# Dense tiles 1 to 4 instead of 2 to 5 in a hybrid decoder layer with a PEER expert FFN

## The chip, the cores and the metric

The kernel runs on one core of a Trainium2 chip. The metric is the device time of one execution in microseconds. Five engines matter here: TensorE (PE, with its weight loads as PEld), VectorE (DVE), ScalarE (ACT), GpSimd (POOL) and SyncE (SP). Each engine runs its own queue of instructions in order. SP, ACT and POOL also issue DMA transfers.

## What is computed

One decoder layer on 1024 tokens of width 1024, then a final norm. A mixer (mLSTM and stick-breaking attention) and a cross-attention into 256 memory tokens come first. The PEER FFN follows: each token picks 128 experts (8 heads, 16 each) out of 16384, and sums them.

```python
def peer_ffn(h, wq, subkeys, u, v):                 # cut
    q = (xt @ wq).reshape(T, PEER_HEADS, 2, PEER_HALF)
    s = jnp.einsum('thpc,hpnc->thpn', q, subkeys)
    ...                                             # top 16 of 256 candidates in each head
    gates = jax.nn.softmax(best, axis=-1)
    def block(args):                                # 128 tokens
        xb, eb, gb = args
        ub = u[eb]
        vb = v[eb]
        act = jax.nn.gelu(jnp.einsum('cd,ced->ce', xb, ub), approximate=False) * gb
        return jnp.einsum('ce,ced->cd', act, vb)
```

`u` and `v` are 16384 rows of 1024 float32 each, 4 KB a row.

## The kernel before, in words

The 1024 tokens are eight tiles of 128. They go through the front (projections, mixers, cross-attention, routing) in five groups, `GROUPS = (1, 2, 2, 1, 2)`: tile 0; tiles 1, 2; tiles 3, 4; tile 5; tiles 6, 7. While one group is in its mixers or in `post`, the projections (`part_a`) and the mixers of the next group are filled in.

After `route`, `topk` (L682) makes a tile's 128 expert numbers `idx` and gates per token. Then there are two ways to compute a tile's experts.

A **gathered** tile (`experts`, L760) runs on POOL and DVE. For each of its 128 slots POOL issues one indirect DMA (L777) that brings one row of `u` for each of the 128 tokens (512 KB) into one of five buffers `uv` (`uvb=5`), DVE multiplies and sums it into `act` (L784), a Gelu and the gate follow, and for each slot a second gather brings the rows of `v`, which DVE adds to `y` (L792). A tile so needs 256 gathers. The `u` gathers run 32 slots ahead of the `v` gathers.

A **dense** tile is computed against all 16384 experts by TensorE. Its gates are first scattered into a matrix `G_scr` in DRAM, zeroed at the start: `topk` issues 128 indirect DMAs (L748), 16 for each of the 8 heads, which add a gate at expert and token. The 16 of one head are declared independent; the first of a head waits until all of the head before it has landed. Then `dense` (L857) goes over 128 blocks of 128 experts for the four dense tiles together (N = 512): `hmat` (L839) loads a block of `u` transposed and makes the activations `h` (24 matmuls, L850), `gpart` loads that block's part of `G_scr` (L875) and multiplies (L876), `vpart` loads the block of `v`, and `ypart` (L896) adds to seven PSUM banks and, for the eighth, through `h` to `y8` in SBUF (L899). The loads of `G_scr` wait for the last scatter of all dense tiles. `split` (L832) makes high and low parts (L834 on ACT, L836 on DVE). The activations may run `ring=12` blocks ahead.

At the end of each tile `finish` (L802) adds the residual, norms and stores.

The order of the instructions on each engine is fixed when the program is built: the tile framework's planner (`schedule_with_timeline_sim=True`) lays all instructions out on a modelled time line, with priority by their place in the program, and `keep_in_program_order`, `declare_no_dep` and the manual order of PE inside `dense` limit it. In program order `experts` comes last, after `dense`, for the tiles that aren't dense in rising number; the scatters stand in `topk`. The buffers `idx` and `gate` are four each (L722, L723).

## Time and profile before

| | us |
|---|---|
| runs shown | 3691.51, 3686.97, 3682.38 |
| median | 3686.97 |
| span of the profiled execution | 3682.8 |

The profiled execution has no time of its own in the list; its span lies 4.2 us under the median. Busy shares of the span: PE 82%, DVE 66%, POOL 58%, ACT 30%; 992 MB are moved at a mean of 269 GB/s. These shares are means over stages that differ, so stage rows are read first, then the waits of a stage. Times in the rows are us from the start of the span.

### The profile page before, as it was taken

What the parts mean: (1) busy time and instruction counts of PE and PEld (TensorE: products, weight loads), DVE (VectorE), ACT (ScalarE), POOL (GpSimd) and SP (SyncE); (2) the same over time, 40 slices, a digit from 0 to 9 for tenths busy, and PEclk for the clock granted to TensorE, in tenths of its full rate; (3) what the DMA queues carried; (4) which work ended last, traced back from release to release, by engine and by line L of the source; (5) the groups of instructions that cost most, each with busy time, mean ns of one, the idle gap of its engine ahead of it and who ended that gap; (6) DMA issues with size and microseconds to landing.
All of it is one profiled execution on the core that took longest, in us unless ns stands there. A gap on an engine that the chain in (4) does not pass through costs nothing.

```text
span 3682.8 us, 41986 instructions
## 1 busy us (share of the span) xinstructions
PE 3024.6 (82%) x14232; PEld 2481.8 (67%) x14232; DVE 2442.9 (66%) x5088; ACT 1108.1 (30%) x2236; POOL 2135.7 (58%) x1540
## 2 busy tenths in 40 slices
PE   8989999978975656664655655999999999999995
PEld 7777877767765545553444544777888887888884
DVE  0217767799953564435422265999888888888888
ACT  3423434323521212222222212233233233332323
POOL 0000545563368888888888887545555555555554
PEclk9999999989987878886787877999999999999997
DMA  9997999999895757664484656989999999999998
GB/s 295 281 322 239 350 334 343 364 316 330 284 304 130 212 139 182 181 154 103 78 216 104 178 118 179 351 309 344 344 342 343 346 339 327 347 340 345 337 334 297
DMA packets 572592, 992.49 MB, mean 269 GB/s; under 512 B 114392, under 2 KB 370520, under 8 KB 572376
## 3 DMA queue, kind: packets, MB, share of 16 engines
q0 software_dynamic: 221184, 537.23, 45.2%
q1 hardware_dynamic: 332144, 418.62, 34.9%
q10 hardware_dynamic: 19048, 33.96, 2.6%
q8 instruction: 112, 1.84, 0.2%
q14 instruction: 104, 0.85, 0.1%
HBM read 939.04 MB, written 50.59 MB: 269 GB/s over the span
## 4 chain that ended last, share of the span: by engine, by line
PE 25%; POOL 12%; issue 7%; DMA 5%; DVE 3%; ACT 1%; POOLq 0%; DVEq 0%; ACTq 0%
PE h L850 12%; PE y L896 11%; POOL G_scr L748 9%; POOL uv L777 4%; DMA uv<-v_in,idx 2%; PE h L896 2%; DMA G_scr<-gate,idx 1%; DMA uv<-u_in,idx 1%; DVE y L792 1%; DVE uv L784 0%; DVE vl L836 0%; DVE al L880 0%; ACT L123 0%; DVE y L899 0%; DVE ge L876 0%
## 5 line engine op out<-in xcount | busy, mean ns | idle before, releaser
L777 POOL DMA_INDIRECT uv<-u_in,idx x512 | 646.1, 1262 | 879.2 <-DVE idx L730 367.1
L748 POOL DMA_INDIRECT G_scr<-gate,idx x512 | 846.8, 1654 | 156.2 <-issue 151.3
L777 POOL DMA_INDIRECT uv<-v_in,idx x512 | 642.6, 1255 | 491.8 <-DVE act L784 224.3
L792 DVE SCALAR_TENSOR_TENSOR y<-uv,act,y 128x1024 f32<-128x1024 f32 x508 | 651.0, 1282 | 341.6 <-DMA uv<-v_in,idx 339.6
L784 DVE CUSTOM_DVE_ANT_0 uv<-uv,xf 128x1024 f32<-128x1024 f32 x512 | 623.8, 1221 | 367.8 <-DMA uv<-u_in,idx 367.0
L850 PE MATMUL h<-xs,uh 128*128 128x512 f32 x1968 | 619.5, 396 | 33.4 <-DVE y L899 15.3
L850 PEld LDWEIGHTS h<-xs,uh 128*128 128x128 f32 x1968 | 373.2, 190 | 120.0 <-DVE y L899 20.8
L238 PE MATMUL ps<-b,w 128*128 128x256 f32 (+1 forms) x2048 | 406.8, 356 | 32.3 <-ACT pq L670 18.3
L238 PEld LDWEIGHTS ps<-b,w 128*128 128x128 f32 x2048 | 347.7, 201 | 76.9 <-ACT pq L670 19.4
L850 PE MATMUL h<-xs,ul 128*128 128x512 f32 x984 | 388.7, 395 | 7.7 <-DVE ul L836 7.7
L896 PE MATMUL y<-vh,ah 128*128 128x512 f32 x896 | 352.3, 393 | 25.8 <-ACT ah L878 22.7
L834 ACT CAST uh<-ur 128x1024 fp32r<-128x1024 f32 x128 | 134.6, 1052 | 760.8 <-PE h L850 644.5
L896 PE MATMUL y<-vh,al 128*128 128x512 f32 x896 | 352.0, 393 | 1.0 <-DVE al L880 1.0
L896 PE MATMUL y<-vl,ah 128*128 128x512 f32 x896 | 350.3, 391 | 2.2 <-DVE vl L836 2.2
L238 PE MATMUL ps<-hT,w 128*128 128x256 f32 (+1 forms) x1280 | 254.8, 354 | 38.4 <-issue 16.9
L238 PEld LDWEIGHTS ps<-hT,w 128*128 128x128 f32 x1280 | 215.6, 201 | 68.7 <-issue 19.7
L850 PEld LDWEIGHTS h<-xs,ul 128*128 128x128 f32 x984 | 187.6, 191 | 48.4 <-DVE ul L836 8.1
L896 PEld LDWEIGHTS y<-vh,ah 128*128 128x128 f32 x896 | 169.3, 189 | 61.8 <-ACT ah L878 23.1
L250 PE MATMUL ps<-w,hT 128*128 128x256 f32 x768 | 184.8, 395 | 19.7 <-DMA w<-w_in_in 19.2
L836 DVE TENSOR_TENSOR ul<-ur,uh 128x1024 fp32r<-128x1024 f32 x128 | 156.6, 1223 | 63.7 <-ACT uh L834 63.7
L896 PEld LDWEIGHTS y<-vl,ah 128*128 128x128 f32 x896 | 169.2, 189 | 40.2 <-DVE vl L836 3.1
L896 PEld LDWEIGHTS y<-vh,al 128*128 128x128 f32 x896 | 169.1, 189 | 38.8 <-DVE al L880 1.7
(269 smaller groups left out, 4269.9 us busy)
## 6 DMA issues: line engine op xcount, KB each, us to landing
w<-w_in_in SPq DMA_DIRECT2D x140, 512.0 KB, 5.8
ur<-uT_in SPq DMA_DIRECT2D x128, 512.0 KB, 6.2
vr<-v_in SPq DMA_DIRECT2D x128, 512.0 KB, 5.9
w<-peer_wq_in SPq DMA_DIRECT2D x80, 512.0 KB, 5.4
G_scr<-zero SPq DMA_DIRECT2D x256, 128.0 KB, 4.9
G<-G_scr SPq DMA_DIRECT2D x128, 256.0 KB, 6.7
w<-w_out_in SPq DMA_DIRECT2D x40, 512.0 KB, 5.9
w<-wq_in SPq DMA_DIRECT2D x40, 512.0 KB, 5.8
```

The lines of the kernel that those rows point to most:

```text
L238: nc.tensor.matmul(b[:, :T], W[k][:, 128 * (j % 2):128 * (j % 2) + 128], hT[:, k, :T], start=k == 0, stop=k == KC - 1)
L250: nc.tensor.matmul(b[:, 256 * q:256 * q + 256], hT[:, k, 128 * t:128 * t + 128], W[q][k], start=k == 0, stop=k == KC - 1)
L748: d = nc.gpsimd.indirect_dma_start(out=self.G_d, out_offset=bass.IndirectOffsetOnAxis(ap=self.idx[tb][:, k:k + 1], axis=0), in_=self.gate[ ...
L777: nc.gpsimd.indirect_dma_start(out=g, out_offset=None, in_=A[tbl], in_offset=bass.IndirectOffsetOnAxis(ap=self.idx[tb][:, s:s + 1], axis=0))
L784: V.tensor_tensor_reduce(u, u, xf, op0=OP.mult, op1=OP.add, scale=1.0, scalar=0.0, accum_out=act[:, s:s + 1])
L792: V.scalar_tensor_tensor(y, v, act[:, k:k + 1], y, op0=OP.mult, op1=OP.add)
L834: self.nc.scalar.copy(hi, src)
L836: self.nc.vector.tensor_sub(lo, src, hi.bitcast(F32))
L850: nc.tensor.matmul(h[:, :N], a[:, ks], self.xs_[:, x, k, :], start=n == 0, stop=n == 3 * KC - 1)
L896: nc.tensor.matmul(b, a[x][:, ts], v[w][:, qs], start=m == 0 and (j == 0 if acc else i == 0), stop=m == 2 and (j == 127 if acc else i == n ...
```

## The change

Only the list of dense tiles differs. Tile 1 is now scattered into `G_scr` and computed by TensorE, and tile 5 is gathered. The gathered tiles are 0, 5, 6 and 7 (before: 0, 1, 6, 7). The counts stay: 512 scatters, 1024 gathers, 128 dense blocks of 512 columns.

```diff
-        Layer(ctx, tc, A, out[0], S, GROUPS, dense=(2, 3, 4, 5), uvb=5, stb=5, wb=6, ra=(1, 0.6, 0.0), flr=(1, 3, 0),
+        Layer(ctx, tc, A, out[0], S, GROUPS, dense=(1, 2, 3, 4), uvb=5, stb=5, wb=6, ra=(1, 0.6, 0.0), flr=(1, 3, 0),
```

## Rows read from the trace of the kernel before

**Rows 1.** Windows: busy time of each engine in four stages, granted clock, DMA share.

```profile
core 0: us, PE busy (x) PEld busy (x) DVE busy (x) ACT busy (x) POOL busy (x), PEclk, DMA share, GB/s
945.00:1055.60 110.60, 98.22 (x525) 77.25 (x524) 99.84 (x201) 52.35 (x127) 42.88 (x39) 0.95 0.86 295
1055.60:2267.80 1212.20, 729.13 (x3384) 589.62 (x3382) 540.01 (x1759) 283.58 (x651) 1007.41 (x669) 0.79 0.62 152
2267.80:3637.00 1369.20, 1339.56 (x5812) 1096.02 (x5812) 1192.91 (x1513) 410.73 (x529) 775.69 (x571) 0.99 0.94 339
3637.00:3682.80 45.80, 10.27 (x44) 8.18 (x44) 35.28 (x35) 18.57 (x45) 16.43 (x13) 0.66 0.73 251
```

**Rows 2.** The chain that ended last, by line, from the page.

```profile
PE h L850 12%; PE y L896 11%; POOL G_scr L748 9%; POOL uv L777 4%; DMA uv<-v_in,idx 2%; PE h L896 2%; DMA G_scr<-gate,idx 1%; DMA uv<-u_in,idx 1%; DVE y L792 1%; DVE uv L784 0%; DVE vl L836 0%; DVE al L880 0%; ACT L123 0%; DVE y L899 0%; DVE ge L876 0%
```

**Rows 3.** Waits of DVE from 1060 to 2200 us: total, times, longest.

```profile
DVE uv L784 <- DMA uv<-u_in,idx: 272.6, 39, 25.0
DVE y L792 <- DMA uv<-v_in,idx: 260.3, 32, 23.2
```

**Rows 4.** Timelines of POOL, SP and PE around the last scatter.

```profile
2266.07 1.55 POOL L748 DMA_INDIRECT G_scr<-gate,idx  x1 [0.31 <-issue]
...
2269.22 0.80 SPq L875 DMA_DIRECT2D G<-G_scr  x2
...
2277.13 0.80 PE L896 MATMUL y<-vh,ah 128*128 128x512 f32 x1 [22.71 <-ACT ah L878]
```

**Rows 5.** Timeline of POOL: the quickest 20 gathers in a row, and the last two.

```profile
774.26 1.50 POOL L777 DMA_INDIRECT uv<-u_in,idx  x1 [0.30 <-issue]
...
807.93 1.74 POOL L777 DMA_INDIRECT uv<-u_in,idx  x1 [0.30 <-DVE ktop L661]
...
3660.91 1.01 POOL L777 DMA_INDIRECT uv<-v_in,idx  x1 [0.30 <-issue]
3662.23 0.93 POOL L777 DMA_INDIRECT uv<-v_in,idx  x1 [0.30 <-issue]
```

**Rows 6.** Windows of the gathers (L777) alone: POOL busy, clock, DMA share.

```profile
945.00:987.00 42.00, 12.56 (x12) 1.00 0.85 283
...
1055.60:2267.80 1212.20, 160.62 (x157) 0.79 0.62 152
2267.80:3662.50 1394.70, 791.45 (x584) 0.98 0.94 338
```

**Rows 7.** Timeline of DVE: when `idx` of tiles 1, 2, 4 and 5 is written.

```profile
944.22 0.23 DVE L730 CAST idx<-kex 128x128 int32<-128x128 f32 x1
1054.73 0.28 DVE L727 TENSOR_SCALAR idx<-kex,consts 128x128 int32<-128x128 f32 x1
...
1446.75 0.51 DVE L727 TENSOR_SCALAR idx<-kex,consts 128x128 int32<-128x128 f32 x1
...
1820.34 0.28 DVE L727 TENSOR_SCALAR idx<-kex,consts 128x128 int32<-128x128 f32 x1
```

**Rows 8.** The scatters on POOL: durations min/median/max, and their group of the page.

```profile
L748 POOL DMA_INDIRECT G_scr<-gate,idx x512: 1542/1542/3750, 1055.7 to 2266.1; - x171
...
L748 POOL DMA_INDIRECT G_scr<-gate,idx x512 | 846.8, 1654 | 156.2 <-issue 151.3
```

**Rows 9.** Timeline of POOL where one head ends and the next begins.

```profile
1084.45 1.54 POOL L748 DMA_INDIRECT G_scr<-gate,idx  x1 [0.30 <-DMA G_scr<-gate,idx]
1086.30 1.00 POOL L777 DMA_INDIRECT uv<-u_in,idx  x1 [0.31 <-issue]
...
1092.59 2.03 POOL L748 DMA_INDIRECT G_scr<-gate,idx  x1 [0.30 <-issue]
```

**Rows 10.** The chain, in order of time: start, us, what; a head's last scatter and its landing.

```profile
1810.17 0.30 issue
1810.48 2.94 DMA G_scr<-gate,idx
```

**Rows 11.** DMA issues: engine, op, count, median us from issue to landing.

```profile
uv<-u_in,idx POOLq DMA_INDIRECT x512, 6.8
```

## Prediction

> **What bounds the kernel now.** I read the stage windows first, then the waits of the stage where the change lies, then single heads on POOL. The windows [rows 1] show three regimes. Up to 1055 us the front runs on a busy PE (98 of 111 us just before). From 1056 to 2268 us POOL is busy 1007 of 1212 us, while PE has 729, DVE 540 and the DMA share falls to 0.62. From 2268 to 3637 us PE is busy 1340 of 1369 us, DVE 1193, and DMA stands at 0.94. The reader is to see that the middle stage is POOL's alone: the rest of POOL's time there is the 0.30 us between instructions. The chain [rows 2] says the same: the scatters and the dense matmuls are its largest parts.
>
> Why does the front, which needs no scatter, crawl in the middle? The waits of DVE [rows 3]: 272.6 + 260.3 = 533 us, in 71 waits, are waits for tile 1's gathers. These stand on POOL behind the scatters, and DVE's fixed order mixes them with the front's work. So the front is paced by POOL there. The dense products can't start before the last scatter: it is issued at 2266.1, `G_scr` is loaded at 2269.2, the first y product runs at 2277.1 [rows 4]. At the other end PE and the gathers finish together: the dense stage ends near 3637, the last gather is issued at 3662.2 [rows 1, 5].
>
> **The change, step by step.**
>
> *What moves.* Tile 1's 256 gathers are removed, of which 440 - 256 = 184 ran before 2268 (1024 - 584 = 440 gathers had been issued, tile 0's 256 among them) [rows 6]. Tile 1's 128 scatters are added and can start when its `idx` is there, at about 945 instead of 1055.7 for tile 2's [rows 7, 8]. Tile 5's scatters go, and its 256 gathers come, after its `idx`. Counts of all instructions stay, so only the places of idle time change.
>
> *Pitch of a head with gathers.* 1212.2 us for 32 heads [rows 1] is 37.9; I use 37.8. The gathers stand there for a reason [rows 9]: after a head's 16th scatter the next head waits for the landing, and five gathers fill the gap.
>
> *Pitch of a head without.* Before tile 5's `idx` there is nothing to fill with, except the 12 gathers that tile 0 still has after 945 [rows 6]. The gap is then the landing: 0.30 + 2.94 us, with the wake-up about 3.4 [rows 10], where the five gathers now take 6.6 (1092.59 - 1085.99) [rows 9]. Scatters last 1.542 us at best and 1.654 on average [rows 8]. With the floor a head is 16 x 1.542 + 15 x 0.30 + 3.4 = 32.6; with the average 34.4. I take 34.0, near the average, since DVE is no idler there.
>
> A rule of the Trainium skill bears on that excess: SBUF — State Buffer, section Who interferes with whom, says that a DVE instruction with two SBUF inputs keeps a GpSimd instruction that reads SBUF waiting. The trace agrees at least in that the floor and the mean differ by 0.11 us [rows 8]. By the rule the heads during which DVE is stalled would run at the floor, and 20 of them would save 28 us of the sum below.
>
> *How many of each.* DVE's own work per head is 37.8 us less its stall: 1140 / 37.8 = 30.2 heads in the window [rows 3], 533 / 30.2 = 17.7, so 20.1 us. I take this as the pace at which the planner laid the front beside the heads. Tile 5's `idx` came 765 us after the first scatter [rows 7], 20 heads; the scatters now begin 110 us earlier, 5.5 heads by that pace, and a front without tile 1's gathers gains some two heads. So about head 23 of 32 tile 5's gathers begin to fill the gaps: 9 heads with 45 gathers. Together with three heads of tile 0's gathers there are 12 heads at 37.8 and 20 at 34.0. The scatters end at 945 + 453.6 + 680 = 2078.6, **189 us earlier** than 2267.8. Tiles 2 to 4 are routed early enough: tile 4's `idx` at 1446.8 or sooner, needed after 24 heads near 1770 [rows 7].
>
> *The front.* It runs free of tile 1's gathers, but this buys nothing by itself: its next partner on DVE is tile 5's gather, which POOL reaches only after some 23 heads. DVE stalls there instead, and the front ends near the last scatter. I let the dense stage start 50 us later against the last scatter than now; bounds 0 and 110.
>
> *The late part.* At 2078.6 there remain 768 - 45 = 723 gathers, where before 584 remained [rows 6]: **139 more**. The dense stage ends at 2078.6 + 1369 + 50 = 3498. In that stage a gather took 1394.7 / 584 = 2.39 us [rows 6]; DVE (87% busy) and DMA (0.94) leave little more [rows 1]. So 1419 / 2.39 = 594 gathers fit, and 129 are left for a tail without the dense work. The trace has no such tail. Bounds: the last gathers, with nothing else, follow at 1.32 us; the dense pace is 2.39. Nearest is the quickest run of 20 beside a light front, 33.7 / 20 = 1.68 [rows 5]. The tail takes 129 x 1.68 = 217 us: last gather at 3715, and the 20.6 us from there to the end (3682.8 - 3662.2) give **3736**, 53 over the span, or 1.4%.
>
> *At nothing.* One tile stored for gathering (`xf_scr`) or dense (`xT_scr`) in `route` is swapped for another; two operations off the chain. The four `finish` calls of dense tiles hide under the tail; uncovered they'd cost what now follows 3637, under 46 us [rows 1].
>
> **The rivals.**
>
> A. *Faster: the planner packs the dense stage tighter.* Three gathered tiles are then ready during dense work, so POOL's and DVE's order there can hold more gathers per block. For it: DVE is idle 176 us of that stage [rows 1]. Against it: DMA at 0.94 [rows 1], and the order was equally free before, with two tiles ready. At 2.15 us a gather 660 fit, 63 are left, the end is 3498 + 106 + 21 = 3625. The point at which it decides is 53 / 1.68 = 32 more gathers in the stage, a pace of 2.27.
>
> B. *No change: the tail runs at POOL's own pace.* At 1.32 us the 129 gathers take 170 and the end is 3689. For it: the last gathers [rows 5]. Against it: five buffers, and 6.8 us from issue to landing over the whole run [rows 11], which with DVE's turn allows one gather in about 1.6 us.
>
> C. *Slower still: the tail is no quicker than the dense stage.* The gather is then held by its buffers and landing, not by dense work: 129 x 2.39 = 308, end 3827. Against it: the 1.68 stretch.
>
> That the change does nothing is excluded: 139 gathers and 32 heads change places.
>
> **How the numbers follow.** Other bounds move the sum by: pitch 32.6 or 34.4, -28 or +8; dense start 0 or 110, -15 or +18 (30% of a shift, since gathers go on meanwhile); 15 or 7 heads with gathers, -28 or +9. The likeliest case is 3736 + 4 (median over span) = 3740, with its own range 3695 to 3790 and a chance of 0.44; A 0.26, B 0.12, C 0.18. Differences under 0.3%, 11 us, can't be told from none. So slower 0.44 + 0.18 = 0.62, same 0.12, faster 0.26. The range reaches from near A's 3629 to near C's 3831 and leaves out their outer halves: 3640 to 3815.
>
> **What would show it.** Right: first scatter near 945; heads of 33 to 35 us without gathers between them, then five in each gap after tile 5's `idx`; last scatter between 2040 and 2110; DVE's long wait for `uv` sits once, before POOL reaches tile 5; PE ends near 3500 and 60 to 170 gathers run after it. Wrong: last scatter before 2030 or after 2150; gathers between heads from the start; more than 625 gathers inside the dense stage; PE and gathers ending together again.

## The result: 2.6% slower

The changed kernel takes 3784.71 us (median of 4 runs, 3778.63 to 3785.91); the kernel before, run beside it, 3689.06. The ratio is 1.0261, 95% interval 1.0246 to 1.0276. The direction was forecast, and the time lies inside the range, but the change costs about twice what was said: the profiled span is 3784.1 us against 3736 in the sum. A learner can follow where the 48 us come from, since every stage can be read off the trace after.

The page of the kernel after, in 40 slices of 94.6 us (busy tenths; the last row is the granted clock of TensorE):

```profile
PE   8989999979789998200166888899999999999940
...
DVE  0217767799627536100124898999888888888886
...
POOL 0000545463877777777887445554556555555666
PEclk9999999989889998655588999999999999999975
```

PE and DVE have a hole in slices 17 to 20 that the kernel before didn't have; POOL works on right through it. The windows of the kernel after show the same by stage (columns as in [rows 1]):

```profile
945.00:1540.00 595.00, 534.62 (x2770) 431.89 (x2768) 325.73 (x1175) 224.17 (x546) 456.74 (x291) 0.92 0.64 146
1540.00:1875.00 335.00, 0.00 (x0) 0.00 (x0) 0.00 (x0) 0.00 (x0) 263.60 (x172) 0.50 0.22 2
1875.00:2024.00 149.00, 96.19 (x372) 75.03 (x372) 42.48 (x70) 41.22 (x93) 124.38 (x81) 0.79 0.65 156
2024.00:2238.00 214.00, 164.63 (x730) 137.47 (x731) 181.75 (x533) 59.17 (x125) 113.52 (x92) 0.89 0.91 326
2238.00:3640.00 1402.00, 1358.02 (x5851) 1109.80 (x5850) 1221.71 (x1619) 415.03 (x534) 789.83 (x585) 0.98 0.93 335
3640.00:3784.10 144.10, 1.49 (x7) 0.91 (x5) 104.97 (x111) 19.44 (x46) 92.77 (x72) 0.52 0.83 292
```

Six stages. The front runs freely. Then, for 335 us, nothing runs but POOL's scatters and, at the very end, three gathers. The front goes on, with tile 5's gathers among it, until the last scatter and beyond it; the dense products start only 214 us after that scatter. Then come the dense stage and a tail almost without PE, which is 144 us where the kernel before had 46 [rows 1]. What the hole waits for stands in DVE's waits from 945 to 2150 us of the kernel after (total, times, longest):

```profile
DVE uv L784 <- DMA uv<-u_in,idx: 423.5, 23, 341.5
DVE y L792 <- DMA uv<-v_in,idx: 47.9, 10, 16.6
```

One single wait of 341.5 us, for tile 5's first gather. Before, there were 71 short ones of 533 us together [rows 3]. The gather does not wait for the routing of tile 5. On DVE its `idx` is written at 1520.66, and on POOL its first gather starts at 1871.40, 0.31 us after a scatter: eleven more heads of scatters stand before it in POOL's order.

```profile
1520.66 0.25 DVE L730 CAST idx<-kex 128x128 int32<-128x128 f32 x1
```

```profile
1871.40 1.01 POOL L777 DMA_INDIRECT uv<-u_in,idx  x1 [0.31 <-issue]
```

The gathers of the kernel after, counted in its last three stages (POOL busy, clock, DMA share, GB/s; compare [rows 6]):

```profile
2024.00:2238.00 214.00, 113.48 (x91) 0.89 0.91 326
2238.00:3640.00 1402.00, 789.83 (x585) 0.98 0.93 335
3640.00:3765.00 125.00, 92.52 (x72) 0.52 0.90 316
```

748 are left when the scatters end (584 before). They go at 2.35, 2.40 and, in the tail, 1.74 us each.

### The profile page after: what moved, and what is told of

Its sections match the earlier page's. It is cut to its first block, busy times and chain, and to the rows that moved or that the text cites. A ratio compares the mean times of both kernels' runs of the same rounds, so it can differ in the third digit from the quotient of the medians.

```text
span 3784.1 us, 42150 instructions
## 1 busy us (share of the span) xinstructions
PE 3002.7 (79%) x14232; PEld 2466.1 (65%) x14232; DVE 2450.5 (65%) x5088; ACT 1105.4 (29%) x2234; POOL 2126.8 (56%) x1540
## 5 line engine op out<-in xcount | busy, mean ns | idle before, releaser
L777 POOL DMA_INDIRECT uv<-u_in,idx x512 | 659.9, 1289 | 888.1 <-DVE idx L730 367.7
L777 POOL DMA_INDIRECT uv<-v_in,idx x512 | 654.8, 1279 | 525.2 <-DVE act L784 238.1
L748 POOL DMA_INDIRECT G_scr<-gate,idx x512 | 812.0, 1586 | 224.8 <-issue 147.6
L850 PE MATMUL h<-xs,uh 128*128 128x512 f32 x1968 | 628.5, 401 | 69.9 <-DVE y L899 40.2
L238 PE MATMUL ps<-b,w 128*128 128x256 f32 (+1 forms) x2048 | 397.2, 350 | 22.6 <-ACT pq L670 9.2
L544 PE MATMUL pz<-sq,consts 128*128 128x512 f32 x144 | 82.9, 660 | 357.2 <-DVE sq L533 356.7
L544 PEld LDWEIGHTS pz<-sq,consts 128*128 128x128 f32 x144 | 25.9, 206 | 367.8 <-DVE sq L533 361.4
```

Of the source, the lines that this page charges most:

```text
L238: nc.tensor.matmul(b[:, :T], W[k][:, 128 * (j % 2):128 * (j % 2) + 128], hT[:, k, :T], start=k == 0, stop=k == KC - 1)
L544: nc.tensor.matmul(z, self.c[:, C_TRI:C_TRI + 128], sp, start=False, stop=False, skip_group_check=True)
L748: d = nc.gpsimd.indirect_dma_start(out=self.G_d, out_offset=bass.IndirectOffsetOnAxis(ap=self.idx[tb][:, k:k + 1], axis=0), in_=self.gate[ ...
L777: nc.gpsimd.indirect_dma_start(out=g, out_offset=None, in_=A[tbl], in_offset=bass.IndirectOffsetOnAxis(ap=self.idx[tb][:, s:s + 1], axis=0))
L850: nc.tensor.matmul(h[:, :N], a[:, ks], self.xs_[:, x, k, :], start=n == 0, stop=n == 3 * KC - 1)
```

## The experiments

The theory to test: the end is the moment of the last scatter, plus the work that must come after it (dense products and remaining gathers, which share DVE and DMA, then a tail of gathers). Gathers put into the gaps between heads are cheap; the stalls of the front cost little by themselves. The rival: the front's stall behind POOL is what costs, so a freed front would give the loss back, and more.

**e1: take the stall away, in the kernel after.** The token rows `xf` of tile 5 get memory that is free only when the front is done, so its sums can't be placed before that on DVE.

```diff
-        xf = gp.tile([128, D], F32, name="xf", bufs=1)
+        xf = (self.dp if tb == 5 else gp).tile([128, D], F32, name="xf", bufs=1)
```

> The kernel after, with the token rows xf that tile 5's sums read placed in memory that the front frees at its end, so that the fixed order can't put tile 5's sums between the front's work on DVE. Nothing is left out. Theory (the time is set by how many gathers stay for after the last scatter; the front's 341 us stall only moves when the dense products start): last scatter near 2015 as before, DVE's long wait gone, front done before 1850, first y product near 2030 instead of 2238; the dense stage ends about 200 us earlier, near 3415, but some 180 gathers instead of 72 are left for a tail at 1.74 us; span near 3750, about 35 us under the kernel after, still slower than the kernel before. Rival 1 (the late start of the dense products is the whole loss): the end moves with the start, span near 3585. Rival 2 (the tail is no quicker than the dense stage, 2.40 us a gather): span near 3860.

Measured: 3748.02 us, ratio to the kernel before 1.0181 (1.016 to 1.0202), span 3745.5. The last scatter is at 2005.2 and the first y product at 2063 instead of 2238. Gathers of e1, in the stages behind the last scatter:

```profile
2005.50:2063.00 57.50, 32.44 (x21) 0.78 0.93 337
2063.00:3494.00 1431.00, 827.55 (x606) 0.98 0.93 336
3494.00:3726.00 232.00, 176.06 (x136) 0.51 0.90 315
```

The dense products now start 175 us earlier and end 146 us earlier, but 136 gathers instead of 72 are left behind them, at 1.71 us. The span falls by 39 us. Rival 1 (3585) and rival 2 (3860) are both out. So of the 101 us that the change costs in the span, taking the stall away gives back 39; by the medians, each against the kernel before run beside it, 28 of 96. The larger part stays without any stall. The edit moves a little more than the stall: the last scatter comes 17 us earlier, and 763 gathers are left instead of 748. The expected span (3750) came out, but not its parts: 180 gathers were expected behind a dense stage ending near 3415.

How far the waits for gathers, which stand behind scatters on POOL, hold up the front shows in its last projections (first and last start), in the kernel before, the kernel after and e1:

```profile
L238 PE MATMUL ps<-b,w x2048: 272/379/797, 26.3 to 2145.3; 128*128 128x256 f32 x117, 128*128 128x128 f32 x70
L238 PE MATMUL ps<-b,w x2048: 272/379/634, 25.9 to 2156.1; 128*128 128x256 f32 x117, 128*128 128x128 f32 x70
L238 PE MATMUL ps<-b,w x2048: 272/379/635, 25.9 to 1740.0; 128*128 128x256 f32 x117, 128*128 128x128 f32 x70
```

The change left the end of the front where it was, near 2150; freed, it ends at 1740.

**e2: the same in the kernel before.** Its 533 us of DVE waits for tile 1's gathers are taken away by the same edit with `tb == 1`.

> The kernel before, with tile 1's xf placed the same way, so that tile 1's gathers run only after the front and its scatters. Nothing is left out. Theory (gathers between the heads fill POOL's gaps nearly free; the 533 us that DVE waits for them cost nothing by themselves): DVE's waits go and the front ends 300 us or more before the last scatter; heads shrink from 37.8 to about 32.5, last scatter near 2095 instead of 2266; 763 gathers instead of 584 remain, dense ends near 3490 and 180 gathers follow; span near 3825, 140 us slower than the kernel before. Rival (the coupling of the front to POOL is what costs): a free front makes it faster than the kernel before, about 3510 to 3600.

Measured: 3794.96 us, ratio 1.031 (1.0284 to 1.0335), span 3795.3. The scatters of e2 (min/median/max, first and last start) and its gathers behind them:

```profile
L748 POOL DMA_INDIRECT G_scr<-gate,idx x512: 1541/1542/2219, 1014.6 to 2058.0; - x171
```

```profile
2058.00:2116.60 58.60, 32.41 (x21) 0.81 0.91 326
2116.60:3545.00 1428.40, 838.65 (x607) 0.98 0.93 336
3545.00:3776.00 231.00, 168.33 (x136) 0.51 0.90 315
```

The front is free and the last scatter comes 208 us earlier than in the kernel before, yet the kernel is 3% slower: 763 gathers instead of 584 are left (one that runs across a boundary stands in two windows). The rival is refuted on this kernel. The expectation was 30 us too high; the last scatter was expected near 2095, and it came 37 us earlier, after a first scatter that moved to 1014.6 as well.

**e3: half of the scatters.** The kernel after issues 8 of the 16 scatters of each head; half of the gates are left out.

```diff
-                for k in range(16 * h, 16 * h + 16):
+                for k in range(16 * h, 16 * h + 8):
```

> The kernel after with only 8 of the 16 scatters of each head issued; half of the gates are left out of G_scr. Theory (POOL's scatters set the middle stage): a head takes about 18 us, the last scatter is near 1530 instead of 2022, DVE's stall of 341 us is gone, tile 5's gathers run beside the front, dense starts near 1900 and span is near 3330 to 3400. Rival (the middle is bound by the front or by DMA, and POOL's backlog only shows there): last scatter earlier, but dense still starts after 2150 and the span stays over 3650.

Measured (one run): 3390.25 us. Scatters and gathers of e3:

```profile
L748 POOL DMA_INDIRECT G_scr<-gate,idx x256: 1541/1555/2791, 951.5 to 1550.3; - x128
```

```profile
1550.50:1900.00 349.50, 181.72 (x145) 0.86 0.91 319
1900.00:3292.00 1392.00, 788.38 (x579) 0.99 0.93 335
3292.00:3370.00 78.00, 56.06 (x44) 0.54 0.91 323
```

The last scatter comes 472 us earlier and the span falls by 396. The longest DVE wait for `uv` there is 50.8 us. So the scatters set the middle stage, not the front and not the rest of the DMA. Half the scatters take away POOL's time and their own DMA together, so e3 alone doesn't part these two; in the 335 us where only the scatters run, POOL is busy 264 us and the DMA share is 0.22.

**e4: fill the gaps with other scatters.** Scatters of different tiles touch different columns of `G_scr` and are declared independent, so heads of two tiles alternate.

```diff
-              vrb=2, gb=2, yw=2).build()
+              vrb=2, gb=2, yw=2, xt=512).build()
```

> The kernel after, with the scatters of different tiles declared independent (their columns of G_scr differ), so that heads of two tiles can alternate and the landing of one hides under the next. Nothing is left out. Theory (each head without gathers pays a gap of about 3.4 us for the landing before it): where two tiles are ready heads take 29.6 instead of 32 to 33 us, the last scatter comes 50 to 100 us earlier, DVE's stall shrinks by as much, span 3690 to 3740. Rival (the queue of the scatters itself is the pace, no gap): last scatter within 15 us of 2022, span 3784.

Measured: 3735.5 us, ratio 1.0155 (1.0131 to 1.0179), span 3731.0. A boundary between two heads of the kernel after, then the scatters of both kernels, e4 last:

```profile
1712.34 1.54 POOL L748 DMA_INDIRECT G_scr<-gate,idx  x1 [0.31 <-issue]
1716.15 1.54 POOL L748 DMA_INDIRECT G_scr<-gate,idx  x1 [2.27 <-DMA G_scr<-gate,idx]
```

```profile
L748 POOL DMA_INDIRECT G_scr<-gate,idx x512: 1541/1542/2639, 945.7 to 2022.5; - x171
```

```profile
L748 POOL DMA_INDIRECT G_scr<-gate,idx x512: 1541/1542/2579, 946.7 to 1958.3; - x171
```

The idle 2.27 us at the boundary is the landing of the head before. In e4 most starts of heads follow each other in 29.5 to 31 us, where the kernel after mostly has 31.4 to 35.4. The last scatter moves by 64 us, the span by 53 (by the medians, each against the kernel before beside it, 40). The expected shrinking of the stall did not come: DVE's long wait is still 327.1 us, 14 less, and the first y product, at 2202, comes 36 us earlier.

**e5: e1 and e4 together.**

> The two edits of e1 and e4 together on the kernel after: tile 5's sums kept behind the front, and heads of different tiles independent. Nothing is left out. Theory (the end is the last scatter plus the work that stays for after it, 763 gathers in both e1 and here): the last scatter comes about 70 us before e1's 2005 us and the span falls by as much, to 3675, level with the kernel before. Rival 1 (the gains of e1 and e4 are one and the same, both shorten the stall): span as e4, 3730. Rival 2 (the dense products are bound by the end of the front): first y product stays near 2060 and the span at 3745.

Measured: 3693.18 us, ratio to the kernel before 1.0011 (0.9996 to 1.0025): level with it. The last scatter is at 1944.5, 61 us before e1's, the first y product at 2002, and the span is 3683.2, 62 us under e1's: here the last scatter carries the end with it one to one. Rivals 1 and 2 are out. In e1, e2 and e5 the front is done in time and 763 gathers are left, and all three end 1736 to 1739 us after the end of the last scatter, which is what the theory asks for.

**e6: e5 with more gather buffers.** Tiles 6 and 7 get three more, from memory of the dense stage.

```diff
-        ... uvb=5, stb=5, ...
+        ... uvb=5, uvx=3, stb=5, ...
```

> e5 with three more gather buffers for tiles 6 and 7 in memory that is free in the dense stage (eight instead of five). Nothing is left out. Theory (the tail's 1.70 us a gather is the time from issue to landing over five buffers): the tail goes at about 1.5 us and the dense stage takes some gathers more; 25 to 40 us less than e5, about 3640, faster than both kernels by 1%. Rival (DMA, busy 0.90 in the tail and 0.94 in the dense stage, is the limit): within 10 us of e5.

Measured: 3627.84 us, ratio 0.9828 (0.9797 to 0.9859): 1.7% faster than the kernel before, and faster than both kernels. Gathers in the dense stage and the tail, of e5 and then of e6:

```profile
2002.00:3440.00 1438.00, 835.78 (x610) 0.98 0.93 335
3440.00:3665.00 225.00, 169.70 (x134) 0.51 0.91 319
```

```profile
2015.00:3446.00 1431.00, 828.86 (x629) 0.98 0.94 344
3446.00:3609.00 163.00, 127.33 (x114) 0.52 0.99 376
```

The tail goes at 1.43 us a gather instead of 1.68, with DMA at 0.99, and 19 gathers more fit into the dense stage. The gain over e5 is 65 us in the medians, more than the 25 to 40 expected; with five buffers the tail was held by them, not by DMA. With eight, DMA is at 0.99; whether more buffers would still help was not tried.

**e7: another tile gathered.** `dense=(1, 2, 3, 5)`; tile 4, whose `idx` comes earlier, is gathered.

```diff
-        ... dense=(1, 2, 3, 4), ...
+        ... dense=(1, 2, 3, 5), ...
```

> The kernel after with tiles 1, 2, 3 and 5 dense, so that tile 4 is gathered; its idx is there at about 1276 us instead of 1520 for tile 5's. Nothing is left out. Theory (gathers in the gaps between heads are cheap, and what counts is how many stay for after the last scatter and when that is): 17 heads and one longer break take 142 gathers, the last scatter is near 2220 with 626 left; DVE's long wait shrinks under 200 us; span 3715 to 3735, between the two kernels. Rival (which tile is gathered only matters through the long stall): no long stall, span at or below the kernel before.

Measured: 3729.47 us, ratio 1.0108 (1.0079 to 1.0137). As counted, 626 gathers are left; the last scatter starts at 2203.4, the dense products at 2289. The longest wait of DVE for a gather, from 1300 to 2210 us of e7:

```profile
DVE uv L784 <- DMA uv<-u_in,idx: 404.9, 34, 179.8
```

It lies between the kernels as the theory said. Fewer gathers are left than in the kernel after, but the last scatter is later. The rival's condition, no long stall, did not come about, so e7 leaves the rival untested.

**e8 and e9: only the buffers,** `uvx=3` in the kernel before and in the kernel after.

> The kernel before with the three more gather buffers of e6 for tiles 6 and 7. Nothing is left out. Theory (before, PE ends the dense stage with 13 gathers left, so quicker gathers have nothing to shorten): within 0.4% of the kernel before. Rival (the gathers' buffers hold up the dense stage through DVE's order): 1% faster or more.

> The kernel after with the three more gather buffers of e6 for tiles 6 and 7, and no other edit. Nothing is left out. Theory (after the change the gathers end last, 125 us behind the dense products, so quicker gathers shorten it, unlike the kernel before): 30 to 60 us less, 3725 to 3755. Rival (the buffers of e6 help only once the dense stage starts early): within 10 us of 3784.

Measured: e8 3693.53 us, ratio 1.0004 (0.9991 to 1.0018), no change; e9 3733.03 us, ratio 1.0125 (1.0096 to 1.0154), 52 us under the kernel after (49 if each median is taken against the kernel before run beside it). In e8 the last y products, then the last gathers (first and last start):

```profile
L896 PE MATMUL y<-vh,ah x896: 387/389/795, 2288.0 to 3675.2; 128*128 128x512 f32 x180
```

```profile
L777 POOL DMA_INDIRECT uvx<-v_in,idx x120: 935/1218/2282, 2460.1 to 3633.0; - x120
```

Quicker gathers end 42 us before PE does, and bring nothing. After the change the gathers end last, and the same buffers pay, even without e1's edit: the rival of e9 is out.

## Why the prediction was right, and where its size failed

**What bounds the middle** was right: e3 moves the end by 396 us by scatters alone.

**The first scatter** was right: it starts at 945.73 (said: near 945). **The heads** were taken too slow. The scatters took 1078 us instead of 1133, so the last starts at 2022.5, not 2077; the prediction had named a last scatter before 2030 as a sign of being wrong. The 24 heads without gathers behind them took 32.6 us each on average, the floor figure and not the 34.0 taken: 34 of the 55 us. The rest comes from the count, seven heads with gathers behind them instead of twelve.

Two terms of a head were too long. The gap to the next head was 2.1 to 2.4 us in the hole, where 3.4 was taken. And the scatter itself was taken near the average before, 1.654 [rows 8]: in the hole, where DVE stands still, 169 scatters take 260.7 us, 1.54 each. Here the rule that was weighed, in the Trainium skill, SBUF — State Buffer, section Who interferes with whom, fits the trace better than the average that was taken: in the kernel after, the 277 scatters during which DVE runs nothing take 1.543 us on average, the 235 others, beside DVE instructions of every kind, 1.636. But more DMA runs beside these others too (share 0.64 from 945 to 1540, 0.22 in the hole), and no run here parts the two.

**How many heads get gathers** was right in kind and wrong in number. Tile 0's last 11 came after the first three heads, then none, then five in each gap; but tile 5's stand in four gaps only, 20 gathers where 45 were forecast, so 748 were left instead of 723. The forecast went by the time at which tile 5's `idx` would be there, near head 23. It was there sooner, at the 17th head, but POOL's order put the first gather only after the 28th.

**DVE's long wait** was foreseen with its place and reason; its length was not worked out.

**The step that failed in size** is the front: "the front ends near the last scatter. I let the dense stage start 50 us later against the last scatter than now", with bounds of 0 and 110. Now it is 9.5 us [rows 4], so the sum held 60; it measured 214 (2024 to 2238), outside the bounds. The wait ended at 1875, and by then 281 us of front were left: its last projections on PE run to 2156, and the first y product comes 82 us later. The sum had the stall but not the work behind it. Nor did PE end near 3500, as the prediction had named for a sign of being right; it ended near 3640. With 60 in place of 214 and all else as measured, the dense stage would end at 2024 + 60 + 1402 = 3486; 1462 / 2.39 = 612 gathers fit, 136 are left at 1.74, and the span would be 3486 + 237 + 20 = 3743, where e1, without the stall, has 3745.5. That is 41 of the 48 us.

That the rest is so small is luck. By the same sum the scatters' earlier end takes 55 us away; 25 more gathers left, a dense stage of 1402 us where the sum held 1359, and the tail's pace give back about 63.

**The late part** was right in its paces: 2.39 us a gather in the dense stage (2.40 measured), 1.68 in the tail (1.74). The tail holds 72 gathers, inside the 60 to 170 given; the sum had 129, but 676 gathers ran between the last scatter and the end of the dense stage, where it had 594.

**The rivals.** A, more gathers packed into the dense stage, did not come: 585 in it, the pace of before. B, a tail at 1.32, is out; five buffers hold it at 1.7 (e5 against e6). C, a tail as slow as the dense stage, is out.

Why the change costs time, then: before, 157 gathers of tile 1 sat in the gaps between heads and 27 ahead of them [rows 6]. With tile 1 scattered, the gaps stay empty until POOL's order reaches tile 5, and 164 gathers more come after the last scatter. At the tail's 1.74 us they cost 285 us, more than the 244 us by which the scatters end earlier. The late front adds the 28 to 39 us that e1 gives back.

What stays open is why the planner put tile 5's first sums where it did on DVE. Its modelled times were not read; that the real scatters run slower than it counts on is an inference from the order and the waits.

## What to carry to other kernels

Moving work to an engine earlier helps only if that engine's gaps stay filled: count what used to fill them and where it must go now. A wait inside a fixed order moves all the work behind it on that engine; when placing a stall, add the work that is still to come after it. And ask which of two streams ends last before buying buffers for one: three buffers were worth nothing before the change and some 50 us after it.

## What the runs showed of the hardware

- The granted clock fell to 0.50, TensorE's lower level of 1.2 GHz, over the 335 us in which PE ran nothing, and stood at 0.79 in the stage after it, where PE was busy 96 of 149 us.
- An indirect scatter takes 1.54 us of POOL's time again and again while DVE is still; over the whole kernel before, the mean was 1.654 [rows 8]. The landing that the next head waits for was seen as 2.27 us of idle in that quiet stretch, where the prediction had estimated a gap of 3.4 from a landing of 2.94 [rows 10].
- In the tails, where almost nothing but gathers moves data, they reached 315 to 323 GB/s with five buffers (DMA share 0.90 to 0.91; after, e1, e2, e3, e5) and 376 GB/s with eight (0.99; e6).
